# Zero-padded 128-row ones products for rotary squares, and a list scheduler with operation times and pairwise hand-over delays

## The chip, the cores and the metric

One Trainium2 chip, all eight NeuronCores. Each core runs the same program on its own queries of a decoder block. The metric is device time in microseconds (us) of the slowest core. Executions come in two states: fast, and slow (the cores of a die, or of both, run at a lower granted TensorE clock in some executions, whatever the kernel).

## The reference, cut to what matters

The block has two parallel mixers and a feed-forward part. The change touches the attention mixer and the way its instructions are ordered:

```python
# q, k have 128 plain and 64 rotary dimensions per head; both are RMS-normalised over all 192
q = apply_rope_tail(rmsnorm(q, q_norm_g[l]), cos, sin)
k = apply_rope_tail(rmsnorm(k, k_norm_g[l]), cos, sin)
y_mla = causal_block_attention(q, k, v) @ w_mla_out[l]      # 16 heads, 4096 keys
y_conv = (zb * causal_dwconv3(zc * zv, conv_w[l])) @ w_conv_out[l]
h = h + (gate_a * y_conv + gate_b * y_mla) @ w_o[l]
# then h = h + W_down(silu(a_g) * a_u): not touched
```

The normalisation needs sums of squares over 128 + 64 dimensions. Dimensions lie on partitions, so the kernel sums with a TensorE product against a matrix of ones.

## The kernel before: the parts that matter

The program is recorded by a Python scheduler. Most of it is emitted in a fixed order. The attention stage is not: seven streams of small units (scores, PV products, block 0, K, V and Q projections of the next head, and the convolution mixer) are merged by a greedy list scheduler. It keeps a modelled clock per engine and places, as TensorE's next unit, the one whose modelled stall is least (in buckets of 0.1 us), with ties broken by a planned position.

```python
LATENCY = {PE: 0.2, ACT: 0.22, DVE: 0.17, POOL: 0.2, SP: 0.0}
...
        t = max([self.free[eng]] + [self.seen[id(d)] for d in o.deps])
        self.free[eng] = t + (0.05 if is_dma else cost)
        self.seen[id(o)] = t + cost + (2.0 if is_dma else LATENCY[eng])
...
    def act(out, in_, func, reads, writes, **kw):
        c = width(out) / 1200.0 + 0.19 + (0.0 if isinstance(kw.get("scale", 1.0), float) else 0.09)
...
# choice of TensorE's next unit
            stall = max(0.0, t - S.free[PE])
            key = (int(stall / 0.1), u.pos)
# choice of the next ScalarE or VectorE instruction: the scores' stream (prio 0) has a head start
                key = (t - (0.3 if prio == 0 else 0.0), prio)
```

The two products with 64 rows (`QS` runs 48 times, in attention; `krstat` 16 times, in the first stage, which makes the keys' latents and ends near 260 us):

```python
# QS: query statistics
            mm(PS[p][:, 0:n], ones, sqn[:, 0:n], True, False, [Tones, Tsqn], [TP[p]])
            mm(PS[p][:, 0:n], ones[0:64, :], sqr[0:64, 0:n], False, True, [Tones, Tsqr], [TP[p]])
# krstat: rotary-key statistics, two one-column products
            mm(PS[BKV][:, 256 + bb:257 + bb], sqkr[0:64, bb * 128:(bb + 1) * 128], ones[0:64, 0:1], True, True,
               [Tsqkr, Tones], [TP[BKV]])
```

Of the kernel before, what the change touches and what calls it, by code (L numbers as in the profile page):

```python
# [13 lines left out]
PE, ACT, DVE, POOL, SP = "tensor", "scalar", "vector", "gpsimd", "sync"  # L14
ENGS = (PE, ACT, DVE, POOL, SP)


LATENCY = {PE: 0.2, ACT: 0.22, DVE: 0.17, POOL: 0.2, SP: 0.0}


class T:
# [28 lines left out]
class Sched:  # L50
# [18 lines left out]
        t.prev = over  # L69
        return t  # L70

    def ready(self, reads, writes):

        t = 0.0
        for x in reads:
            if x.w is not None:
                t = max(t, self.seen[id(x.w)])
        for x in writes:
            for o in ([x.w] if x.w is not None else []) + x.r:
                t = max(t, self.seen[id(o)])  # L80
        return t

    def add(self, eng, fn, reads=(), writes=(), chan=None, cost=0.1):
        is_dma = chan is not None
        if self.rec is not None and eng != PE and eng != POOL:
            self.rec.append((eng, fn, reads, writes, chan, cost))
            return None
        o = Op(eng, fn, is_dma, chan)
        deps = {}

        def consider(d):
            if d is None or d is o:
                return
            if not d.is_dma and not is_dma and d.eng == eng == PE:
                return
            deps[id(d)] = d

        for t in reads:
            assert not t.dead, t.name
            consider(t.w)  # L100
            if t.excl:
                for r in t.r:
                    if r.eng != eng:
                        deps[id(r)] = r
        for t in writes:
            assert not t.dead, t.name
            if t.prev:
                stack = list(t.prev)
                while stack:
                    p = stack.pop()  # L110
                    p.dead = True
                    consider(p.w)
                    for r in p.r:
                        consider(r)
                    if p.prev:
                        stack += p.prev
                t.prev = None
            consider(t.w)
            for r in t.r:
                consider(r)  # L120
        if is_dma:
            consider(self.chan_last.get(chan))
            self.chan_last[chan] = o
        for t in reads:
            t.r.append(o)
        for t in writes:
            t.w = o
            t.r = []
        o.deps = list(deps.values())
        t = max([self.free[eng]] + [self.seen[id(d)] for d in o.deps])  # L130
        self.free[eng] = t + (0.05 if is_dma else cost)
        self.seen[id(o)] = t + cost + (2.0 if is_dma else LATENCY[eng])
        if is_dma:
            c = self.chan_cnt.get(chan, 0) + 1
            self.chan_cnt[chan] = c
            o.done_val = 16 * c
        self.ops[eng].append(o)
        return o
# [151 lines left out]
def build_program():  # L290
# [22 lines left out]
    S = Sched(nc)  # L313
# [58 lines left out]
    def width(ap):  # L372
        n = 1
        for d in ap.shape[1:]:
            n *= d
        return n

    def mm(out, lhsT, rhs, start, stop, reads, writes):
        S.add(PE, lambda e: e.matmul(out, lhsT=lhsT, rhs=rhs, start=start, stop=stop), reads, writes,  # L379
              cost=max(width(rhs) / 2400.0, 0.055) + 0.003)  # L380

    def act(out, in_, func, reads, writes, **kw):
        c = width(out) / 1200.0 + 0.19 + (0.0 if isinstance(kw.get("scale", 1.0), float) else 0.09)
        S.add(ACT, lambda e: e.activation(out=out, in_=in_, func=func, **kw), reads, writes, cost=c)  # L384

    def dcost(out, *ins):
        fast = all(x.dtype == BF16 for x in (out,) + ins)
        return width(out) / (1920.0 if fast else 960.0) + 0.065

    def stt(out, in0, scalar, in1, op0, op1, reads, writes):  # L390
        S.add(DVE, lambda e: e.scalar_tensor_tensor(out=out, in0=in0, scalar=scalar, in1=in1, op0=op0, op1=op1),  # L391
              reads, writes, cost=dcost(out, in0, in1))

    def tt(out, in0, in1, op, reads, writes):
        S.add(DVE, lambda e: e.tensor_tensor(out=out, in0=in0, in1=in1, op=op), reads, writes,  # L395
              cost=dcost(out, in0, in1))

    def ts(out, in0, s1, s2, op0, op1, reads, writes):
        c = dcost(out, in0)
        if s2 is None:  # L400
            S.add(DVE, lambda e: e.tensor_scalar(out=out, in0=in0, scalar1=s1, scalar2=None, op0=op0), reads, writes,  # L401
                  cost=c)
        else:
            S.add(DVE, lambda e: e.tensor_scalar(out=out, in0=in0, scalar1=s1, scalar2=s2, op0=op0, op1=op1),  # L404
                  reads, writes, cost=c)
# [152 lines left out]

    S.add(DVE, lambda e: e.memset(ones, 1.0), writes=[Tones])  # L559
    S.add(DVE, lambda e: e.memset(krope[64:128, :], 0.0), writes=Tkr)  # L560
    INV2PI = 1.0 / (2.0 * math.pi)
    C1 = 6.28125
    C2 = 2.0 * math.pi - 6.28125
# [82 lines left out]

    def krstat(g):
        for bb in range(2):
            mm(PS[BKV][:, 256 + bb:257 + bb], sqkr[0:64, bb * 128:(bb + 1) * 128], ones[0:64, 0:1], True, True,
               [Tsqkr, Tones], [TP[BKV]])  # L650
        cp(krss[:, 2 * g:2 * g + 2], PS[BKV][:, 256:258], [TP[BKV]], [Tkrss])

# [137 lines left out]
    Tgd = [T("gd%d" % i) for i in range(8)]  # L790
    for i_ in range(2):
        S.add(DVE, lambda e, i_=i_: e.memset(Qr[i_][64:128, :], 0.0), writes=[TQr[i_]])  # L792


    class Unit:
# [82 lines left out]
    def prologue_units(h):  # L878
# [66 lines left out]
        def QS(t):  # L945
            off, n = QT[t]
            p = fbank()
            mm(PS[p][:, 0:n], ones, sqn[:, 0:n], True, False, [Tones, Tsqn], [TP[p]])
            mm(PS[p][:, 0:n], ones[0:64, :], sqr[0:64, 0:n], False, True, [Tones, Tsqr], [TP[p]])
            rsq(rsqh[:, 0:n], PS[p][:, 0:n], 192.0, [TP[p]], [Trsqh])  # L950

            stt(Qn[hb][:, off:off + n], qraw[:, 0:n], gqe, rsqh[:, 0:n], ALU.mult, ALU.mult,
                [Tqraw, Tgqe, Trsqh], [TQn[hb]])
            tt(Qr[hb][0:64, off:off + n], qr_[0:64, 0:n], rsqh[0:64, 0:n], ALU.mult, [Tqr_, Trsqh], [TQr[hb]])
# [235 lines left out]
    def bank_choice(stream):  # L1190
        allowed = [6, 7]
        if pos["qk"] < 0:
            allowed = [0, 1, 2, 3, 4, 5, 6, 7]
        else:
            if 20 <= pos["qk"] % 32 <= 27:
                allowed += [1, 3]
            if 19 <= pos["pv"] % 32 <= 28 and pos["fin"] >= 2 * (pos["pv"] // 32):
                allowed.append(4)
        allowed = [b for b in allowed if free_(b)]
        if stream is st_c and not [b for b in (6, 7) if free_(b) and b != allowed[-1]]:  # L1200
            return None, 0.0
        if not allowed:
            return None, 0.0
        rt = {b: S.ready([], [TP[b]]) for b in allowed}
        b = min(allowed, key=lambda b: (max(rt[b], S.free[PE]), b in (6, 7), b))
        return b, rt[b]

    def post(horizon, once=False):

        while True:  # L1210
            best = None
            for prio, s in enumerate(streams):
                if not s.pend:
                    continue
                e, fn, rd, wr, ch, c, marks, bank = s.pend[0]
                t = max(S.free[e], S.ready(rd, wr)) if e in (ACT, DVE) else 0.0
                key = (t - (0.3 if prio == 0 else 0.0), prio)
                if best is None or key < best[0]:
                    best = (key, t, s)
            if best is None or (best[1] > horizon and not once):  # L1220
                return best is not None
            once = False
            s = best[2]
            e, fn, rd, wr, ch, c, marks, bank = s.pend.pop(0)
            S.add(e, fn, rd, wr, ch, c)
            for name, v in marks:
                pos[name] = v
            for b in bank:
                owner[b] -= 1
            if s is st_b and not s.pend:  # L1230
                pos["b"] = s.done - 1
# [52 lines left out]
    while any(s.units for s in streams):  # L1284
        post(S.free[PE] + 0.6)
        best = None
        for s in streams:
            if not s.units:
                continue
            u = s.units[0]  # L1290
            if len(s.pend) > 5 or (u.strict and s.pend) or (u.ok and not u.ok()):
                continue
            t = S.ready(u.need, []) if s is not st_s else S.ready([], u.need)
            bk_ = None
            if u.bank:
                bk_, tb = bank_choice(s)
                if bk_ is None:
                    continue
                t = max(t, tb)
            stall = max(0.0, t - S.free[PE])  # L1300
            key = (int(stall / 0.1), u.pos)
            if best is None or key < best[0]:
                best = (key, s, bk_)
# [263 lines left out]
```

## Time and profile before

Median 2770.38 us of 3 runs (2767.91 to 2771.78). These lines are the engines' busy times and the chain that ended last, from the page of the kernel before (core 6, the slowest; 110 of its 18722 TensorE records are missing):

```profile
PE 2624.4 (95%) x18612; PEld 1652.4 (60%) x18722; DVE 1637.5 (59%) x3248; ACT 891.9 (32%) x1598; POOL 172.3 (6%) x300
...
PE 80%; DVE 6%; issue 5%; ACT 4%; DMA 3%; SPq 1%; DVEq 0%; ACTq 0%; POOLq 0%
```

TensorE is busy 95% of the time and is 80% of the chain: only what TensorE does not spend streaming can be gained. The next lines are groups by shape of TensorE on core 3 (columns: operation, active rows * columns of the array, shape, count, then busy us, mean ns, and idle time just before with what ended it):

```profile
L379 PE MATMUL ps<-arena 128*128 128x348 bf16 x416 | 79.0, 316 | 3.5 <-DVE arena L391 1.4 <-DVE arena L408 0.8 <-ACT arena L384 0.8
...
L379 PE MATMUL ps<-arena 64*128 64x348 bf16 x32 | 10.2, 318 | 0.0
L379 PE MATMUL ps<-arena 64*128 64x344 bf16 x16 | 5.1, 317 | 0.0
L379 PE MATMUL ps<-arena 64*128 64x1 bf16 x32 | 3.0, 160 | 9.3 <-ACT arena L384 9.3
```

The busy time per product, 79.0/416 = 0.19 us for full-row products and 10.2/32 = 0.32 us for 64-row ones, must not be read as their cost: a group's busy time counts overlap only within the group, and each 64-row product of 348 columns stands alone between full-row ones. (The one-column 64-row products, which come in pairs, show 3.0/32 = 0.09 us at a mean of 160 ns.) The cost shows in the start times of single records (kernel before, core 3, a product with the two around it):

```
start us   active rows x columns    to the next start
442.891    128 x 390                0.164
443.055    128 x 348                0.242   <- next has 64 rows
443.297     64 x 348                0.250   <- next has 128 rows
443.547    128 x 128                0.066
```

Between full-row products of 348 columns the step is 0.147 us.

From the same records I split each core's attention stage (first 512-column product to last 456-column product) into streaming time (columns at 2.4 per ns, a one-column product counted as 25 ns, which is about its step), half-clock time, the extra 0.095 and 0.103 us at 64-row products, and all other gaps over 20 ns, called waits. The rest, called small, is a nanosecond or so per product. Means of the six cores whose records were complete:

```
kernel before     us
stage             986.3
streaming         877.6
half clock          3.8
64-row steps        9.6
waits              78.1   (301 of them)
small              17.2
```

This is the waits view of TensorE over that stage, kernel before, core 3 (columns: who waited for whom, total us, times, longest; only gaps over 0.15 us, counted from the modelled end of the product before, so that they add up to less than the waits). The L numbers are helpers: L384 activations, L395 tensor-tensor, L408 copies, L391 scalar-tensor-tensor.

```profile
PE ps L379 <- ACT arena L384: 17.3, 45, 1.6
PE ps L379 <- DVE arena L395: 10.1, 27, 1.1
PE ps L379 <- DMA arena<-wall: 7.6, 1, 7.6
PE ps L379 <- DVE arena L408: 4.7, 9, 1.2
PE ps L379 <- DVE arena L391: 4.5, 6, 1.5
...
```

There is no single culprit; many small waits on ScalarE and VectorE.

### The profile page before, as it was taken

The numbers are of one execution on the slowest core, as the hardware profiler recorded it, in microseconds if no ns is written. First come the engines' busy times: TensorE is split into PE (matmuls) and PEld (weight loads), VectorE is DVE, ScalarE is ACT, GpSimd is POOL, SyncE is SP. The second block draws the span as 40 slices with busy tenths as digits, with TensorE's granted clock in tenths as the row PEclk, the third lists the DMA queues.
The fourth block names the chain that finished last, engine by engine and source line by source line (L and its number), as shares of the span: only waits on it lengthen the run. The fifth ranks groups of instructions, "written<-read, shape, count | busy, mean of one in ns | idle before, by whom it ended". The sixth has DMA issues, their size and how long they took to land.

```text
span 2770.5 us, 51821 instructions; the slowest of 8 cores (2758.7 to 2770.5 us)
## 1 busy us (share of the span) xinstructions
PE 2624.4 (95%) x18612; PEld 1652.4 (60%) x18722; DVE 1637.5 (59%) x3248; ACT 891.9 (32%) x1598; POOL 172.3 (6%) x300
## 2 busy tenths in 40 slices
PE   3899899999999999999999999999999999999997
PEld 2777555565565555555666666666646646655653
DVE  5774477878887888886111112247727745754762
ACT  3553366656656666664111112320000000000000
POOL 0000000000000000000000000001111011111100
PEclk9999899999999999999999999999999999999999
DMA  9552302020212020215444447444454444444445
GB/s 239 162 171 45 59 18 41 15 41 15 47 18 45 15 41 15 34 42 123 76 72 80 73 75 175 97 73 74 69 83 77 72 74 84 74 69 81 76 87 142
DMA packets 67113, 205.65 MB, mean 74 GB/s; under 512 B 7600, under 2 KB 7856, under 8 KB 66736
## 3 DMA queue, kind: packets, MB, share of 16 engines
q0 software_dynamic: 42624, 135.94, 29.7%
q1 hardware_dynamic: 24240, 66.38, 7.3%
q8 instruction: 157, 2.57, 0.4%
q14 instruction: 92, 0.75, 0.1%
HBM read 321.34 MB, written 14.78 MB: 121 GB/s over the span
## 4 chain that ended last, share of the span: by engine, by line
PE 80%; DVE 6%; issue 5%; ACT 4%; DMA 3%; SPq 1%; DVEq 0%; ACTq 0%; POOLq 0%
PE ps L379 80%; ACT arena L384 4%; DVE arena L395 3%; DMA outT<-arena 2%; DVE arena L391 2%; DVE arena L408 1%; DMA arena<-arena 1%; SPq L411 0%; DVE arena L401 0%; DMA arena<-wall 0%; DVEq L183 0%; ACTq L183 0%; DVE arena L404 0%; DVE arena L560 0%; DVE arena L792 0%
## 5 line engine op out<-in xcount | busy, mean ns | idle before, releaser
L379 PE MATMUL ps<-arena 128*128 128x390 bf16 (+10 forms) x18612 | 2624.4, 299 | 133.4 <-ACT arena L384 81.7
L379 PEld LDWEIGHTS ps<-arena 128*128 128x128 bf16 x18722 | 1652.4, 98 | 1104.9 <-issue 263.3
L395 DVE TENSOR_TENSOR arena<-ps,arena 128x390 f32<-128x390 f32 (+6 forms) x760 | 380.5, 508 | 830.8 <-PE ps L379 716.4
L395 DVE TENSOR_TENSOR arena<-arena 128x512 bf16<-128x512 bf16 (+20 forms) x1458 | 625.6, 474 | 95.6 <-ACT arena L384 69.2
L384 ACT ACTIVATE arena<-ps,arena 128x128 bf16<-128x128 f32 (+10 forms) x672 | 436.2, 672 | 478.0 <-PE ps L379 433.7
L384 ACT ACTIVATE arena<-arena 128x390 bf16<-128x390 f32 (+11 forms) x374 | 227.6, 636 | 898.7 <-DVE arena L391 788.5
L391 DVE SCALAR_TENSOR_TENSOR arena<-arena 128x256 bf16<-128x256 f32 (+8 forms) x583 | 419.7, 755 | 90.2 <-ACT arena L384 67.4
L384 ACT ACTIVATE arena<-ps 128x512 bf16<-128x512 f32 (+13 forms) x547 | 248.5, 472 | 375.3 <-PE ps L379 371.3
L411 POOL DMA_DIRECT2D arena<-wall x294 | 170.9, 582 | 2562.1 <-PE ps L379 2327.7
L408 DVE CAST arena<-ps 128x512 bf16<-128x512 f32 x128 | 87.9, 687 | 45.8 <-PE ps L379 44.4
L404 DVE TENSOR_SCALAR arena<-arena 128x1024 f32<-128x1024 f32 (+1 forms) x90 | 72.3, 803 | 2.6 <-ACT arena L384 2.5
L391 DVE SCALAR_TENSOR_TENSOR arena<-ps,arena 128x256 bf16<-128x256 f32 x64 | 26.5, 476 | 48.8 <-ACT arena L384 48.8
L408 DVE COPY arena<-ps 128x456 f32<-128x456 f32 (+2 forms) x64 | 27.1, 424 | 1.4 <-DVE arena L395 0.5
L401 DVE TENSOR_SCALAR arena<-arena 128x390 f32<-128x390 f32 (+7 forms) x36 | 20.5, 570 | 7.9 <-DMA arena<-arena 5.4
L384 ACT ACT_TABLE_LOAD x5 | 6.4, 1283 | 33.7 <-DVE arena L401 15.5
L395 DVE TENSOR_TENSOR arena<-arena,ps 128x390 bf16<-128x390 f32 (+1 forms) x24 | 12.3, 511 | 2.4 <-PE ps L379 1.5
L408 DVE COPY arena<-arena 128x6 f32<-128x6 f32 (+2 forms) x32 | 9.4, 293 | 2.0
L560 DVE MEMSET arena<- 64x4096 bf16 x1 | 3.5, 3472 | 0.9 <-issue 0.9
L408 DVE CAST arena<-arena 128x1028 f32<-128x1028 int32 (+1 forms) x5 | 3.5, 697 | 0.4
L792 DVE MEMSET arena<- 64x1040 bf16 x2 | 1.9, 925 | 0.4 <-issue 0.4
L559 DVE MEMSET arena<- 128x128 bf16 x1 | 0.2, 165 | 1.2 <-PEq L291 1.2
L411 POOL DMA_DIRECT2D arena<-wkvin x1 | 0.7, 664 | 0.9 <-POOLq L291 0.9
(5 smaller groups left out, 0.9 us busy)
## 6 DMA issues: line engine op xcount, KB each, us to landing
arena<-wall POOLq DMA_DIRECT2D x182, 512.0 KB, 5.8
arena<-xg SPq DMA_DIRECT2D x64, 512.0 KB, 5.2
arena<-wall POOLq DMA_DIRECT2D x64, 352.0 KB, 4.5
arena<-xo SPq DMA_DIRECT2D x16, 520.0 KB, 24.7
arena<-wall POOLq DMA_DIRECT2D x32, 256.0 KB, 3.8
outT<-arena SPq DMA_DIRECT2D x32, 256.0 KB, 3.0
arena<-wall POOLq DMA_DIRECT2D x16, 384.0 KB, 5.1
att_d<-arena SPq DMA_DIRECT2D x16, 260.0 KB, 2.1
```

The source lines that it names most:

```text
L379: S.add(PE, lambda e: e.matmul(out, lhsT=lhsT, rhs=rhs, start=start, stop=stop), reads, writes, cost=max(width(rhs) / 2400.0, 0.055) + 0.003)
L384: S.add(ACT, lambda e: e.activation(out=out, in_=in_, func=func, **kw), reads, writes, cost=c)
L391: S.add(DVE, lambda e: e.scalar_tensor_tensor(out=out, in0=in0, scalar=scalar, in1=in1, op0=op0, op1=op1), reads, writes, cost=dcost(out, ...
L395: S.add(DVE, lambda e: e.tensor_tensor(out=out, in0=in0, in1=in1, op=op), reads, writes, cost=dcost(out, in0, in1))
L401: S.add(DVE, lambda e: e.tensor_scalar(out=out, in0=in0, scalar1=s1, scalar2=None, op0=op0), reads, writes, cost=c)
L404: S.add(DVE, lambda e: e.tensor_scalar(out=out, in0=in0, scalar1=s1, scalar2=s2, op0=op0, op1=op1), reads, writes, cost=c)
L408: S.add(DVE, lambda e: e.tensor_copy(out=out, in_=in_), reads, writes, cost=dcost(out, in_))
L411: S.add(eng, lambda e: e.dma_start(out=out, in_=in_), reads=reads, writes=writes, chan=chan, cost=2.0)
L559: S.add(DVE, lambda e: e.memset(ones, 1.0), writes=[Tones])
L560: S.add(DVE, lambda e: e.memset(krope[64:128, :], 0.0), writes=Tkr)
L792: S.add(DVE, lambda e, i_=i_: e.memset(Qr[i_][64:128, :], 0.0), writes=[TQr[i_]])
```

## The change

The intent is, first, to make the 64-row products full-row by zeroing the upper 64 partitions once, so that TensorE never changes its row mode (the time lost at such a change is called a drain below); second, to give the scheduler operation times and hand-over delays as traces show them, for each pair of engines, so that its order fits the machine better.

```diff
-LATENCY = {PE: 0.2, ACT: 0.22, DVE: 0.17, POOL: 0.2, SP: 0.0}
+TAIL = {PE: 0.0, ACT: 0.115, DVE: 0.085, POOL: 0.1, SP: 0.0}
+HOP = {PE: 0.147, ACT: 0.1, DVE: 0.1, POOL: 0.15, SP: 0.1}
+HOP_PE = {PE: 0.0, ACT: 0.3, DVE: 0.34, POOL: 0.35, SP: 0.3}
+def lag(o, eng):
+    return HOP[eng] if o.is_dma else HOP_PE[eng] if o.eng == PE else TAIL[o.eng] + HOP[eng]
...
-        t = max([self.free[eng]] + [self.seen[id(d)] for d in o.deps])
+        t = max([self.free[eng]] + [self.seen[id(d)] + lag(d, eng) for d in o.deps])
...
-        c = width(out) / 1200.0 + 0.19 + (0.0 if isinstance(kw.get("scale", 1.0), float) else 0.09)
+        c = width(out) / 1200.0 + (0.055 if any(t.excl for t in reads) else 0.105) + 0.09 * ptr(kw.get("scale", 1.0))
... (VectorE: +0.065 us where a scalar operand is a pointer)
+    S.add(DVE, lambda e: e.memset(sqkr[64:128, :], 0.0), writes=[Tsqkr])
-            mm(PS[BKV][:, 256 + bb:257 + bb], sqkr[0:64, ...], ones[0:64, 0:1], True, True,
+            mm(PS[BKV][:, 256 + bb:257 + bb], sqkr[:, ...], ones[:, 0:1], True, True,
+    S.add(DVE, lambda e: e.memset(sqr[64:128, :], 0.0), writes=[Tsqr])
-            mm(PS[p][:, 0:n], ones[0:64, :], sqr[0:64, 0:n], False, True, [Tones, Tsqr], [TP[p]])
+            mm(PS[p][:, 0:n], ones, sqr[:, 0:n], False, True, [Tones, Tsqr], [TP[p]])
```

(`excl` marks banks of PSUM, the memory that the products write to: reading one makes the modelled activation 0.05 us cheaper.) Apart from the two memsets no instruction is added or removed; the order in the attention stage changes on TensorE, ScalarE and VectorE.

More of the change, by code (lines that the diff above doesn't have):

```diff
@@ L70, in region, with ready @@
         return t
-    def ready(self, reads, writes):
+    def ready(self, eng, reads, writes):
         t = 0.0
@@ L76, in ready @@
             if x.w is not None:
-                t = max(t, self.seen[id(x.w)])
+                t = max(t, self.seen[id(x.w)] + lag(x.w, eng))
         for x in writes:
             for o in ([x.w] if x.w is not None else []) + x.r:
-                t = max(t, self.seen[id(o)])
+                t = max(t, self.seen[id(o)] + lag(o, eng))
         return t
@@ L129, in add @@
         o.deps = list(deps.values())
-        t = max([self.free[eng]] + [self.seen[id(d)] for d in o.deps])
+        t = max([self.free[eng]] + [self.seen[id(d)] + lag(d, eng) for d in o.deps])
         self.free[eng] = t + (0.05 if is_dma else cost)
-        self.seen[id(o)] = t + cost + (2.0 if is_dma else LATENCY[eng])
+        self.seen[id(o)] = t + cost + (2.0 if is_dma else 0.0)
         if is_dma:
@@ L380, in mm @@
               cost=max(width(rhs) / 2400.0, 0.055) + 0.003)
+    ptr = lambda x: 0.0 if x is None or isinstance(x, (int, float)) else 1.0
     def act(out, in_, func, reads, writes, **kw):
-        c = width(out) / 1200.0 + 0.19 + (0.0 if isinstance(kw.get("scale", 1.0), float) else 0.09)
+        c = width(out) / 1200.0 + (0.055 if any(t.excl for t in reads) else 0.105) + 0.09 * ptr(kw.get("scale", 1.0))
         S.add(ACT, lambda e: e.activation(out=out, in_=in_, func=func, **kw), reads, writes, cost=c)
@@ L391, in stt @@
         S.add(DVE, lambda e: e.scalar_tensor_tensor(out=out, in0=in0, scalar=scalar, in1=in1, op0=op0, op1=op1),
-              reads, writes, cost=dcost(out, in0, in1))
+              reads, writes, cost=dcost(out, in0, in1) + 0.065 * ptr(scalar))
     def tt(out, in0, in1, op, reads, writes):
@@ L398, in ts @@
     def ts(out, in0, s1, s2, op0, op1, reads, writes):
-        c = dcost(out, in0)
+        c = dcost(out, in0) + 0.065 * ptr(s1)
         if s2 is None:
@@ L648, in krstat @@
         for bb in range(2):
-            mm(PS[BKV][:, 256 + bb:257 + bb], sqkr[0:64, bb * 128:(bb + 1) * 128], ones[0:64, 0:1], True, True,
+            mm(PS[BKV][:, 256 + bb:257 + bb], sqkr[:, bb * 128:(bb + 1) * 128], ones[:, 0:1], True, True,
                [Tsqkr, Tones], [TP[BKV]])
@@ L1203, in bank_choice @@
             return None, 0.0
-        rt = {b: S.ready([], [TP[b]]) for b in allowed}
+        rt = {b: S.ready(PE, [], [TP[b]]) for b in allowed}
         b = min(allowed, key=lambda b: (max(rt[b], S.free[PE]), b in (6, 7), b))
@@ L1215, in post @@
                 e, fn, rd, wr, ch, c, marks, bank = s.pend[0]
-                t = max(S.free[e], S.ready(rd, wr)) if e in (ACT, DVE) else 0.0
+                t = max(S.free[e], S.ready(e, rd, wr)) if e in (ACT, DVE) else 0.0
                 key = (t - (0.3 if prio == 0 else 0.0), prio)
@@ L1292, in build_program @@
                 continue
-            t = S.ready(u.need, []) if s is not st_s else S.ready([], u.need)
+            t = S.ready(PE, u.need, []) if s is not st_s else S.ready(PE, [], u.need)
             bk_ = None
```

## The prediction

> **What bounds the kernel now.** The page of the profile gives TensorE 2624 us busy of 2770 (95%), and 80% of the chain that ended last; VectorE is at 59%, ScalarE at 32%. Reading the starts of the matmuls one by one, the attention stage (about 313 to 1302 us) lasts 984 to 992 us, of which 878 is pure streaming at the full clock. Gaps over 20 ns beyond streaming time make up 89 to 96 us of the rest: about 12 us is one wait for weights at the start, 5 to 10 us is a half-clock stretch near 310 to 325 us, about 10 us belongs to the 64-row products below, and some 60 us is hundreds of waits of 0.1 to 1.8 us on ScalarE and VectorE. Everything after it is nearly gapless (windows: 99 to 100% busy) and untouched.
>
> **Part 1, padded products.** The groups by form show 80 matmuls and 80 weight loads with 64 active rows: 48 in the query statistics (348 or 344 columns), 32 with one column in the rotary-key statistics. In the timeline a 348-column matmul is followed after 147 ns, but after 242 ns by one of 64 rows, and that one by the next after 250 ns (medians, where no other wait shows): about 95 + 103 ns lost per product. The Trainium skill, "TensorEngine Tiling (Array Packing)", Key Properties, says that changing the tiling mode drains TensorE; this trace agrees in that the next weight load starts only about 0.25 us after the 64-row matmul, instead of during it. 48 x 0.2 = 9.6 us, of which some is hidden where the next matmul waits anyway: 8.5 us. The rotary-key products are followed after 295 ns, where a full-row one-column product takes 25 to 55: about 0.24 us x 16 = 3.8 us. Padding adds no matmul time (64 and 128 rows both take about 320 ns); of two memsets under 0.4 us the second may delay attention by 0.3 us. Sum: about 12 us, all on the critical path.
>
> **Part 2, the schedule.** Instruction counts stay; only the order in the attention stage changes on TensorE, ScalarE, VectorE. The old model was not far off where it matters: QK product to exponential to mask to PV product is 1.76 us in its figures and about 1.76 with traced durations (1.02 us exponential over 912 columns, 0.22 mask, hand-overs 0.10 to 0.15). It overstates ScalarE occupancy by 0.13 us (912 columns: 0.91 traced, 1.04 modelled) and understates evictions by VectorE by about 0.14 us. In the new order, with traced latencies and no queueing, about as many products stand too close behind their producers as before (495 against 518; summed shortfall 153 against 152 us, overlapping). So the waits should shrink only a little: 6 us of the 60, with an uncertainty of 12 either way.
>
> **Predicted time** 2752 us (range 2733 to 2768). Faster by over 2%: 0.04; within 2%: 0.95; slower by over 2%: 0.01.
>
> **What would show it.** 64-row forms vanish; the gaps around the query-statistics products fall to streaming time; the key-latent stage (to 258 us) shortens by 3 to 4 us; the attention stage shortens by 10 to 25 us; everything after it keeps its length. TensorE waits on ScalarE and VectorE in attention fall from about 60 us to 50 to 58.
>
> **What would make it wrong.** The greedy scheduler may fall into a much better or worse order (VectorE is 80% busy there, so queueing decides); a denser TensorE may meet more half-clock time; the drain may hide behind waits that stay.

## The result, and the profile after

The two fast executions took 2773.51 and 2773.72 us (two more, at 3050.81 and 3063.0, were slow: die 0 at a clock of 0.88 to 0.89). The ratio to the kernel before is 1.0014, 95% interval 0.999 to 1.0038: the same. Ratios here are the mean time of one kernel's fast runs over that of the other's of the same rounds, so not quite the ratio of the medians quoted.

The same parts of the page for the changed kernel (core 3, the slowest):

```profile
PE 2628.2 (95%) x18722; PEld 1655.3 (60%) x18722; DVE 1642.1 (59%) x3250; ACT 893.8 (32%) x1598; POOL 172.5 (6%) x300
...
PE 84%; ACT 5%; DVE 5%; issue 4%; DMA 2%; SPq 1%; ACTq 0%; DVEq 0%; POOL 0%; POOLq 0%
```

The groups by shape, core 3. The 64-row groups are gone, 448 = 416 + 32 and 544 = 512 + 32:

```profile
L386 PE MATMUL ps<-arena 128*128 128x348 bf16 x448 | 82.6, 313 | 2.4 <-DVE arena L417 1.9 <-ACT arena L393 0.4
...
L386 PE MATMUL ps<-arena 128*128 128x1 bf16 x544 | 25.7, 164 | 10.2 <-ACT arena L393 9.3 <-DVE arena L417 0.5 <-DVE arena L404 0.2
```

TensorE's waits in the attention stage, core 3 (L393 activations, L404 tensor-tensor, L417 copies, L400 scalar-tensor-tensor):

```profile
PE ps L386 <- ACT arena L393: 15.4, 44, 0.8
PE ps L386 <- DMA arena<-wall: 11.9, 2, 11.7
PE ps L386 <- DVE arena L417: 10.9, 15, 2.1
PE ps L386 <- DVE arena L404: 9.7, 21, 1.2
PE ps L386 <- DVE arena L400: 3.0, 4, 1.8
```

Waits for VectorE's copies went from 4.7 to 10.9 us and the longest from 1.2 to 2.1. The split of the stage, means of the cores with complete records:

```
                  before   after
stage              986.3   988.3
streaming          877.6   877.6
half clock           3.8     6.2
64-row steps         9.6     0
waits               78.1    87.7
small               17.2    16.8
```

So the 9.6 us did vanish, and came back almost to the microsecond as waits (+9.6) and half-clock time (+2.4).

Two details. First, the first stage did not shorten, though its one-column products are full-row now. The timeline around one of them, kernel before and then the changed kernel, both core 6 (start us, duration, engine, instruction):

```profile
222.34 1.27 DVE L391 SCALAR_TENSOR_TENSOR arena<-ps,arena 128x256 bf16<-128x256 f32 x3 [3.46 <-ACT arena L384]
222.62 0.12 PEld L379 LDWEIGHTS ps<-arena 64*128 64x128 bf16 x2 [0.70 <-issue]
222.65 0.81 PE L379 MATMUL ps<-arena 64*128 64x1 bf16 x5 [0.45 <-ACT arena L384]
...
222.94 0.35 PEld L379 LDWEIGHTS ps<-arena 128*128 128x128 bf16 x4 [0.20 <-issue]
```

```profile
226.78 0.87 DVE L400 SCALAR_TENSOR_TENSOR arena<-ps,arena 128x256 bf16<-128x256 f32 x2 [3.46 <-ACT arena L393]
227.06 0.13 PEld L386 LDWEIGHTS ps<-arena 128*128 128x128 bf16 x2 [0.70 <-issue]
227.09 0.59 PE L386 MATMUL ps<-arena 128*128 128x1 bf16 x3 [0.45 <-ACT arena L393]
...
227.38 0.13 PEld L386 LDWEIGHTS ps<-arena 128*128 128x128 bf16 x2 [0.19 <-issue]
```

The weight load that follows starts 0.60 us after VectorE's eviction in both (222.94 - 222.34, 227.38 - 226.78). It belongs to the first product into PSUM bank 0 of the next group, and the first of those evictions (0.48 us by its record) is what frees bank 0: the product waits for a semaphore of VectorE that rises 0.49 us after the start of that eviction in both kernels, and it starts 0.14 us later. The 295 ns step after the one-column products was this wait. For the weight load the profile says only "issue", that is, it names no releaser.

Second, the new order bunches waits. TensorE, ScalarE and VectorE around 712 us of the changed kernel, core 3, and the windows view of the same stretch (columns: window, length, busy time and count for PE, PEld, DVE, ACT, POOL, then granted clock, DMA share, GB/s):

```profile
711.96 1.36 PE L386 MATMUL ps<-arena 128*128 128x348 bf16 x10 [0.99 <-DVE arena L417]
...
714.95 0.29 DVE L417 COPY arena<-ps 128x128 f32<-128x128 f32 x1
...
715.39 7.46 PE L386 MATMUL ps<-arena 128*128 128x128 bf16 x42 [2.07 <-DVE arena L417]
```

```profile
707.00:710.00 3.00, 3.00 (x24) 1.70 (x22) 0.32 (x2) 2.90 (x6) 0.00 (x0) 1.00 0.02 5
710.00:716.00 6.00, 2.94 (x20) 1.61 (x21) 5.69 (x14) 2.54 (x7) 0.53 (x1) 0.88 0.48 64
716.00:722.00 6.00, 6.00 (x35) 3.35 (x34) 2.33 (x5) 1.60 (x4) 0.00 (x0) 0.55 0.24 68
```

VectorE is full (5.69 of 6 us) and a small copy stands in its queue behind other work; TensorE needs that copy and is busy 2.94 of 6 us; then its clock drops to half from 714.5 to 721.3 us. All eight cores show half-clock stretches between 330 and 1250 us of the changed kernel (3.4 to 10.2 us long in sum); of the kernel before, two cores do (3.4 us). The Trainium skill, "TensorE: Matmul & The Clock Gate", Part 1, says that the clock falls to half after an idle window of about 3.4 us. The trace agrees in the direction, with the difference that two shorter gaps (1.2 and 2.2 us, counted from where streaming ends; the view's 0.99 and 2.07 us count from modelled ends) with 1.2 us of products between them were enough.

### The profile page after: what moved, and what is told of

Its sections match the earlier page's. It is cut to its first block, busy times and chain, and to the rows that moved or that the text cites. A ratio compares the mean times of both kernels' runs of the same rounds, so it can differ in the third digit from the quotient of the medians.

```text
span 2771.9 us, 51904 instructions; the slowest of 8 cores (2761.3 to 2771.9 us)
## 1 busy us (share of the span) xinstructions
PE 2628.2 (95%) x18722; PEld 1655.3 (60%) x18722; DVE 1642.1 (59%) x3250; ACT 893.8 (32%) x1598; POOL 172.5 (6%) x300
## 4 chain that ended last, share of the span: by engine, by line
PE 84%; ACT 5%; DVE 5%; issue 4%; DMA 2%; SPq 1%; ACTq 0%; DVEq 0%; POOL 0%; POOLq 0%
PE ps L386 84%; ACT arena L393 5%; DVE arena L404 3%; DMA outT<-arena 1%; DVE arena L400 1%; DVE arena L417 1%; SPq L420 1%; DMA arena<-arena 1%; DMA arena<-wall 0%; DVE arena L410 0%; DMA arena<-cst 0%; ACTq L190 0%; DVEq L190 0%; DVE arena L413 0%; ACT L393 0%
## 5 line engine op out<-in xcount | busy, mean ns | idle before, releaser
L386 PE MATMUL ps<-arena 128*128 128x390 bf16 (+12 forms) x18722 | 2628.2, 300 | 130.6 <-ACT arena L393 79.3
L404 DVE TENSOR_TENSOR arena<-ps,arena 128x390 f32<-128x390 f32 (+6 forms) x760 | 380.8, 508 | 821.5 <-PE ps L386 718.7
L404 DVE TENSOR_TENSOR arena<-arena 128x130 bf16<-128x130 bf16 (+21 forms) x1458 | 632.7, 474 | 120.4 <-ACT arena L393 89.8
L393 ACT ACTIVATE arena<-ps,arena 128x910 bf16<-128x910 f32 (+10 forms) x672 | 438.7, 672 | 501.1 <-PE ps L386 455.4
L393 ACT ACTIVATE arena<-arena 128x390 bf16<-128x390 f32 (+11 forms) x374 | 228.4, 637 | 901.4 <-DVE arena L400 788.8
L400 DVE SCALAR_TENSOR_TENSOR arena<-arena 128x256 bf16<-128x256 f32 (+8 forms) x583 | 419.8, 755 | 95.3 <-ACT arena L393 72.2
L393 ACT ACTIVATE arena<-ps 128x512 bf16<-128x512 f32 (+13 forms) x547 | 247.3, 473 | 350.2 <-PE ps L386 345.4
L417 DVE CAST arena<-ps 128x512 bf16<-128x512 f32 x128 | 87.7, 685 | 18.2 <-PE ps L386 17.3
L400 DVE SCALAR_TENSOR_TENSOR arena<-ps,arena 128x256 bf16<-128x256 f32 x64 | 26.5, 477 | 53.3 <-ACT arena L393 53.3
L417 DVE COPY arena<-ps 128x456 f32<-128x456 f32 (+2 forms) x64 | 27.1, 424 | 1.0
L404 DVE TENSOR_TENSOR arena<-arena,ps 128x390 bf16<-128x390 f32 (+1 forms) x24 | 12.3, 511 | 3.5 <-PE ps L386 2.3
L417 DVE COPY arena<-arena 128x6 f32<-128x6 f32 (+2 forms) x32 | 9.4, 292 | 1.8
L417 DVE CAST arena<-arena 128x1028 f32<-128x1028 int32 (+1 forms) x5 | 3.5, 697 | 0.6 <-DMA arena<-posg 0.2
```

Source lines behind the costliest of these rows:

```text
L386: S.add(PE, lambda e: e.matmul(out, lhsT=lhsT, rhs=rhs, start=start, stop=stop), reads, writes, cost=max(width(rhs) / 2400.0, 0.055) + 0.003)
L393: S.add(ACT, lambda e: e.activation(out=out, in_=in_, func=func, **kw), reads, writes, cost=c)
L400: S.add(DVE, lambda e: e.scalar_tensor_tensor(out=out, in0=in0, scalar=scalar, in1=in1, op0=op0, op1=op1), reads, writes, cost=dcost(out, ...
L404: S.add(DVE, lambda e: e.tensor_tensor(out=out, in0=in0, in1=in1, op=op), reads, writes, cost=dcost(out, in0, in1))
L417: S.add(DVE, lambda e: e.tensor_copy(out=out, in_=in_), reads, writes, cost=dcost(out, in_))
```

## The experiments

Theory 1: the drains' removal is partly absorbed, since products that stood behind a drain then wait for ScalarE or VectorE; and the new order is a somewhat worse draw from a scheduler whose orders scatter. Theory 2: the padding is worth its full 9.6 us, and the new order loses all of it. Later a theory 3: what the scheduler lacks is not accuracy but slack.

Some expectations quote "a replay". That is a small program of mine that runs the recorded order with in-order engines and the traced durations and hand-overs, without drains or half clock. It only helped to choose and to expect.

### pad_only: the padding without the new order

```diff
 (kernel before, plus)
+    S.add(DVE, lambda e: e.memset(sqkr[64:128, :], 0.0), writes=[Tsqkr])
+    S.add(DVE, lambda e: e.memset(sqr[64:128, :], 0.0), writes=[Tsqr])
 (and the two full-row products of the change)
```

> The kernel before with the padded products alone; the order of instructions on TensorE, ScalarE, Pool and the DMA queues is exactly that of before. Theory 1 (the drains stood partly in the way of nothing: products that waited behind a drain now wait for ScalarE or VectorE instead; a replay of the same order with the traced durations and without drains gives waits of 82 us where the trace has 78 plus 9.6 of drains): attention-stage drains 9.6 to 0, waits 78 to about 82, attention 5 us shorter, 2765 us. Theory 2 (drains were fully on the critical path, and the whole loss of the change lies in the new order): waits stay at 78, attention 9 to 10 us shorter, 2760 us. Both: the first stage does not shorten, since the one-column products' successors still start 0.30 us later.

Measured: median of the 5 fast runs 2768.98 us against 2772.78 before; ratio 0.9981 (0.9969 to 0.9994), about 5 us. In attention: stage 980.6 us (-5.7), 64-row steps 0, waits 82.9 (+4.8). The first stage did not shorten (234.3 us, before 232.1; it varies from 230 to 236 between cores). Theory 1 fits: of 9.6 us of drains half came back as waits in the very same order.

That the drains themselves are gone can be read product by product, since the order is the same. This is the place of the table above, in pad_only (core 3):

```
start us   active rows x columns    to the next start
447.437    128 x 390                0.167
447.604    128 x 348                0.147
447.751    128 x 348                0.146   <- was 64 rows
447.897    128 x 128                0.055
```

Over all 48 places on that core the median step beyond streaming fell from 98 to 2 ns before the padded product and from 106 to 2 ns after it.

### model_only: the new order without the padding

```diff
 (changed kernel, minus the two memsets, and back to)
-            mm(PS[p][:, 0:n], ones, sqr[:, 0:n], False, True, [Tones, Tsqr], [TP[p]])
+            mm(PS[p][:, 0:n], ones[0:64, :], sqr[0:64, 0:n], False, True, [Tones, Tsqr], [TP[p]])
 (likewise krstat)
```

> The changed kernel with the 64-row products back; the order on all engines is exactly that of the changed kernel. Theory 1: drains 9.6 back, waits about 4 less than the changed kernel's 88, attention about 993 us, whole run 2777 us. Theory 2: about 998 us in attention, whole run 2782 us. If the new order were better than the old and something else had eaten the gain: below 2770 us.

Measured: median of the fast runs 2782.08 us, ratio 1.0029 (1.0016 to 1.0042), 8 us slower than before. Attention 995.7 us: 64-row steps 9.6, waits 84.6, half clock 6.6. The time lies on theory 2's figure (2782), the waits nearly on theory 1's (84), and the stage between the two (993 and 998). With the first run the effects add up: old to new order costs 9.4 us with 64-row products (995.7 - 986.3) and 7.7 us with padded ones (988.3 - 980.6); padding gains 5.7 in the old order and 7.4 in the new one. So both theories were partly right: padding is worth 6 to 7 us, and the new order loses 8 to 9.

### hop_20ns_less and hop_20ns_more: one constant moved by 20 ns

```diff
-HOP = {PE: 0.147, ACT: 0.1, ...
+HOP = {PE: 0.127, ACT: 0.1, ...       # hop_20ns_less; 0.167 in hop_20ns_more
```

> The changed kernel with one constant of the scheduler's model, the hand-over to TensorE, at 0.127 instead of 0.147 us; nothing else. If the order is a matter of luck at this level (the greedy choice flips everywhere after the first flip), attention changes by several us, and a replay of the order with traced durations says 17 us longer: about 2788 us. If the model's accuracy rules, 20 ns less on 147 should cost no more than 1 to 3 us: 2772 to 2776 us.

> The changed kernel with the hand-over to TensorE at 0.167 instead of 0.147 us. Luck theory: the order scatters by some us whichever way the constant goes; a replay says 5 us longer in attention than the changed kernel: 2772 to 2782 us. If 20 ns less cost 15 us because slack is that steep, 20 ns more should gain about as much: 2758 us.

Measured: 20 ns less, median 2787.60 us, ratio 1.0054 (1.0039 to 1.0069), attention 1005.3 us (+17.0 on the changed kernel). 20 ns more, median 2778.62 us, ratio 1.0006 (0.9953 to 1.0058, made wide by one run of before at 2796), attention 993.5 us (+5.2). Both directions are worse. (The profiled execution of 20 ns more, 2784.43 us, was the slowest of its four fast ones.) I read this as scatter of 5 to 17 us between orders; the 8 us that the new order lost is within it. Two points that are both worse could also mean a narrow optimum at the traced value. margin_40, next, speaks against that: it moves the same constant, with others, 0.4 us away and is far faster.

### margin_40: deliberately less accurate

```diff
-HOP = {PE: 0.147, ...
-HOP_PE = {PE: 0.0, ACT: 0.3, DVE: 0.34, ...
+HOP = {PE: 0.547, ...
+HOP_PE = {PE: 0.0, ACT: 0.7, DVE: 0.74, ...
-                key = (t - (0.3 if prio == 0 else 0.0), prio)
+                key = (t - (0 if prio == 0 else 0.0), prio)
```

> The changed kernel with 0.4 us added to the modelled hand-overs from TensorE to ScalarE and VectorE and from those to TensorE, and the 0.3 us head start of the exponentials' stream in posting removed; deliberately less accurate than the traces. If accuracy is what makes a good order, this must be slower than the changed kernel: over 2775 us. If slack is what makes a good order (a product placed only just behind its producer's modelled end stalls as soon as anything is late), waits in attention fall from 88 to about 45 to 55 us: 2730 to 2742 us.

Measured: median of the fast runs 2723.50 us, ratio 0.9823 (0.9809 to 0.9837). Attention 936.7 us, waits 38.1 us (about 120 of them, where the changed kernel had 347). That is more than the slack theory had expected (2730 to 2742 us, waits 45 to 55). A model that overstates each hand-over with TensorE by 0.4 us, with the head start gone, gives a far better order than the accurate one.

### prio_only and margin_30_only: which half of margin_40

The first takes only the `key` line above; the second only the constants, at 0.447, 0.6 and 0.64.

> The changed kernel with only the 0.3 us head start of the exponentials' stream removed, no added hand-over time: the half of margin_40 that is not slack. If slack made margin_40's gain, this one stays within about 5 to 8 us of the changed kernel (a replay of its order with traced durations: 5 us less in attention): 2762 to 2770 us. If the removed head start made the gain: near 2724 us.

> The changed kernel with 0.3 us added to the modelled hand-overs between TensorE and ScalarE or VectorE, both ways, and the head start kept: slack alone. Slack theory: TensorE waits in attention fall from 88 to about 55 us (replay: 31 us shorter), 2735 to 2745 us. If the head start were what mattered: 2765 us or more.

Measured: prio_only median 2760.01 us, ratio 0.996 (0.9942 to 0.9979), attention 978.4, waits 76.9. margin_30_only median 2735.81 us, ratio 0.987 (0.9848 to 0.9893), attention 948.6, waits 49.7, 161 of them. The slack alone takes 39.7 us off the changed kernel's stage, over twice the scatter seen above; removing the head start is worth 10 us on its own, which is within that scatter. (prio_only came out just below its expected 2762 to 2770 us, margin_30_only within 2735 to 2745.)

### old_model_margin_30: slack on the old model

```diff
 (pad_only, and)
-LATENCY = {PE: 0.2, ACT: 0.22, DVE: 0.17, ...
+LATENCY = {PE: 0.5, ACT: 0.52, DVE: 0.47, ...
 (and no head start)
```

> The kernel before with padded products, its old model, 0.3 us added to the old latencies of TensorE, ScalarE and VectorE, and no head start. If slack works whatever the model, this is clearly faster than padding alone: replay 16 us shorter in attention, about 2750 us. If slack pays only on top of the refined model: 2765 us or more. Since the old latency also lengthens the hand-overs between ScalarE and VectorE, it may pay less than the refined model's margin.

Measured: one fast run of four, 2746.67 us, so no ratio with an interval. Attention on that run 963.1 us, waits 63.7: 17.5 us below pad_only. That agrees with slack helping the old model too but does not show it: the run also removes the head start, worth 10 us in prio_only, and 17 us is what 20 ns on one constant moved. That it gains less than in margin_30_only may come from the hand-overs between ScalarE and VectorE that it also lengthens, or from scatter; no run tells these apart.

### handovers_only: the new hand-overs with the old operation times

```diff
-        c = width(out) / 1200.0 + (0.055 if any(t.excl for t in reads) else 0.105) + 0.09 * ptr(...)
+        c = width(out) / 1200.0 + 0.19 + (0.0 if isinstance(kw.get("scale", 1.0), float) else 0.09)
 (and no pointer term on VectorE)
```

> The changed kernel with the new hand-over delays but the old operation times: ScalarE again costs 0.13 us too much for each instruction that reads PSUM. Slack theory: the refined operation times took away slack that the old ones held by mistake, so with them back the run is faster than the changed kernel: replay of the order 10 us shorter in attention, TensorE waits there about 78, 2760 to 2766 us. If the refined operation times were what kept the change from being worse: above 2774 us.

Measured: median 2756.18 us, ratio 0.9928 (0.9883 to 0.9972, made wide by the same run of before at 2796); attention 974.3 us, waits 74.7, all somewhat better than expected (2760 to 2766 us, waits about 78). That is 14.0 us less than the changed kernel: by this run, of the model's two halves, the refined operation times are what made its order worse, while the new hand-overs gave an order 6.3 us shorter than pad_only's (980.6). The old operation times charged ScalarE 0.13 us too much for an activation out of PSUM; that this kept slack by accident is the reading of theory 3, not shown. Fourteen us is inside the scatter that 20 ns can cause, so this run agrees with theory 3 but would not carry it alone. The opposite half (new operation times, old latencies) could not be tried: the order reads a PSUM bank in the middle of an accumulation group.

### margin_60: the fastest version found

```diff
+HOP = {PE: 0.774, ...
+HOP_PE = {PE: 0.0, ACT: 0.91, DVE: 0.95, ...
+        post(S.free[PE] + 0.8)              # 0.6 in the change
+            key = (int(stall / 0.07), u.pos)  # 0.1 in the change
 (and no head start)
```

> The best of some 1500 settings by a replay of their orders with traced durations: 0.61 to 0.63 us of added hand-over, no head start, posting horizon 0.8, stall buckets of 0.07 us. Replay: 7 us shorter in attention than margin_40, waits about 31 us, 2714 to 2720 us. If gains from slack end near 0.4 us, within 4 us of margin_40's 2724.

Measured: median of the three fast runs 2715.16 us, ratio 0.98 (0.9776 to 0.9823, so whether it is 2% faster is unclear); results correct. It is the pick of some 1500 settings and changes the posting horizon and the buckets too, so its 4.3 us over margin_40 (936.7 - 932.4) say nothing of slack alone. Attention 932.4 us, waits 33.0. TensorE's waits in that stage, core 3, to be read against the two lists above:

```profile
PE ps L386 <- DVE arena L404: 13.6, 29, 0.7
PE ps L386 <- DVE arena L417: 2.8, 2, 2.2
PE ps L386 <- DVE arena L400: 2.3, 2, 1.4
PE ps L386 <- ACT arena L393: 2.1, 6, 0.5
```

Waits for ScalarE fell from 15.4 to 2.1 us and those for VectorE's copies from 10.9 to 2.8; those for its tensor-tensor operations rose from 9.7 to 13.6. The sum rows of the windows view over the attention stage, the changed kernel and then margin_60, core 3:

```profile
sum 986.00, PE 942.44 PEld 578.48 DVE 795.53 ACT 605.41 POOL 27.44; mean PE 942.44 PEld 578.48 DVE 795.53 ACT 605.41 POOL 27.44
```

```profile
sum 932.00, PE 910.73 PEld 586.81 DVE 786.61 ACT 603.88 POOL 27.44; mean PE 910.73 PEld 586.81 DVE 786.61 ACT 603.88 POOL 27.44
```

ScalarE and VectorE do nearly the same work (VectorE 9 us less, ScalarE 1.5 us less) in 54 us less: little was saved on them; what fell is TensorE's waiting for them.

All runs in one table (attention stage, means of the six cores with complete records; streaming is 877.6 and small gaps 17 us in each):

```
kernel                stage   waits  half clock  64-row   fast median
before                986.3    78.1     3.8       9.6     2770.38
changed               988.3    87.7     6.2       0       2773.6
pad_only              980.6    82.9     3.4       0       2768.98
model_only            995.7    84.6     6.6       9.6     2782.08
hop_20ns_less        1005.3   100.0    10.9       0       2787.60
hop_20ns_more         993.5    91.9     7.3       0       2778.62
handovers_only        974.3    74.7     5.3       0       2756.18
prio_only             978.4    76.9     6.9       0       2760.01
old_model_margin_30   963.1    63.7     4.5       0       2746.67 (one run)
margin_30_only        948.6    49.7     4.0       0       2735.81
margin_40             936.7    38.1     3.5       0       2723.50
margin_60             932.4    33.0     4.2       0       2715.16
```

The stage figures are of one profiled execution of each kernel; within one execution the six cores differ by 1.4 to 3.5 us (standard deviation). The medians come from four sessions, in which the fast runs of the kernel before had medians of 2769.6 to 2772.8 us.

## Why the prediction was wrong

It forecast 2752 us (2733 to 2768); the fast runs took 2773.5 to 2773.7. The step that failed most is the order. Where the forecast had 6 us shorter waits, the new order cost 7.7 us (changed against pad_only): 13.7 us of a miss of about 20 (13.7 + 3.8 + 2.8). The rotary-key products are 3.8 us of it (forecast 3.8, measured 0), the query statistics 2.8 (forecast 8.5, measured 5.7). Point by point:

- **The drain at query statistics, "95 + 103 ns lost per product", 9.6 us**: right. The 64-row steps vanished, and steps between 348-column products fell to 0.147 us. The Trainium skill's statement that a change of tiling mode drains TensorE ("TensorEngine Tiling (Array Packing)", Key Properties) agrees with the trace, and now with its absence after padding.
- **"8.5 us" of it gained**: too much. pad_only gained 5.7 us in attention with an unchanged order, since waits rose by 4.8. I allowed only for products that were seen waiting after a drain. I did not allow for the rest of the stage: with TensorE earlier everywhere, later products reach ScalarE and VectorE before these are ready.
- **"about 0.24 us x 16 = 3.8 us" at the rotary-key products**: wrong, it was nothing. The step of 295 ns was put down to the same drain by likeness. It was a wait for VectorE to free bank 0, and it measured 295 ns after padding as well. I had checked what the product itself waits for, and not what its successor waits for.
- **"the waits should shrink only a little: 6 us of the 60"**: wrong in sign. The new order costs 7.7 to 9.4 us (model_only against before, changed against pad_only): about 5 to 6.5 us more of waits and about 2.8 us more at half clock. The "uncertainty of 12 either way" (6 us longer at worst) about covered the waits; my range for the sum, to 2768, did not allow for that together with the overstated padding. The waits were also mis-sized: the wait for weights that I counted within the stage lies before it, so the waits were 78 us, not 60.
- **That the order's quality was near that of the old**: the count of products too close behind their producers (495 against 518) ignored the queues on ScalarE and VectorE. It could not see that TensorE would stand behind a full VectorE queue at 712 us. That the other added waits come from queues as well was not traced one by one.
- **"VectorE is 80% busy there, so queueing decides" and "a denser TensorE may meet more half-clock time"**, the listed risks: both happened, though at 712 us, the stretch that I looked at, half-clock time came from bunched waits, not from density.

What stays open: of the 8 us that the new order loses, the half-clock part can be pointed at, and the refined operation times lose 14 us against handovers_only. But since 20 ns on one constant moves the stage by as much, no single wrong figure of the model can be called the cause.

## What to carry to other kernels

A greedy list scheduler that packs to its modelled times leaves no slack, and here small errors then seem to become stalls of the bottleneck engine: overstating the hand-overs to and from it by 0.3 us was worth 40 us in the attention stage (0.4 and 0.6 us, with other settings changed too, 52 and 56), where making them accurate was worth 6, within the scatter, and making the operation times accurate as well lost 14. Before crediting a scheduler change, move one constant by a trifle and see how far the time scatters. And when a cost on the bottleneck engine is removed, look at what the next instruction waits for: half of a saving on TensorE came back as waits for engines that were busy 61 and 81% of the stage (605 and 796 of 986 us in the changed kernel), and a gap that merely resembled a drain was a wait for a PSUM bank.

## What the Trainium skill lacked or had wrong

- "TensorEngine Tiling (Array Packing)", Key Properties, says that changing the tiling mode drains TensorE but gives no cost: here 95 ns before and 103 ns after a 64-row product of 344 or 348 columns in a stream of full-row ones, and 0 with the rows padded.
- "TensorE: Matmul & The Clock Gate", Why this matters for your kernels, asks to avoid idle gaps of over about 3 us. Taken alone, that was too lenient here: in the changed kernel no gap near 712 us was over 2.3 us (1.2 and 2.2 us, with 1.2 us of products between), and the clock still fell to half for 6.8 us.
- No page that I used gives hand-over delays between engines. Traced here, from an instruction's recorded end to the start of the one that waited for it: ScalarE or VectorE to TensorE 0.14 to 0.15 us, ScalarE to VectorE 0.10 us, TensorE, whose ends are modelled, to ScalarE 0.10 us (medians).
